# HGRN2 recurrence of a hybrid decoder step: the operands of levels 4, 8 and of the first corner copied aside, the level products grouped

## The chip, the cores and the metric

The kernel runs on one core of a Trainium2 chip. The metric is the device time of one execution in microseconds (us), median of the runs. All work is in one program: products on TensorE (PE), elementwise work on VectorE (DVE) and ScalarE (ACT), a little on GpSimd (POOL), and transfers issued mostly by SyncE (SP).

## What is computed

The reference is one step of a two-layer decoder for a prompt of 2048 tokens and 8 sample sequences of 8 tokens. Layer 0 joins a gated DeltaNet with sliding-window attention; layer 1 is an HGRN2 recurrence with 8 heads of 128 x 128 state. The change touches layer 1 alone:

```python
def hgrn2_recurrence(q, k, v, logf, s0):
    # S_t = diag(f_t) S_{t-1} + k_t v_t^T (k_t = 1 - f_t), o_t = S_t^T q_t / sqrt(dk), chunkwise
    ...
    def step(s, xs):
        q_c, k_c, v_c, G_c = xs
        dec = masked_exp(causal, G_c[:, :, :, None, :] - G_c[:, :, None, :, :])
        a = jnp.einsum('nhid,nhijd,nhjd->nhij', q_c, dec, k_c)
        o = jnp.einsum('nhid,nhde->nhie', q_c * jnp.exp(G_c), s) + jnp.einsum('nhij,nhje->nhie', a, v_c)
        gl = G_c[:, :, -1]
        s = s * jnp.exp(gl)[..., None] + jnp.einsum('nhid,nhie->nhde', k_c * jnp.exp(gl[:, :, None] - G_c), v_c)
        return s, o
```

Here `a` is a causal matrix of token by token, in which each pair is damped by the forget gates of the tokens between them, channel by channel.

## The kernel before

All operands of the large products are split into a high and a low part, so that a product is three passes (`product`). These are the **dense** products. They write three PSUM banks (bank_66 to bank_68); everything else writes five more (bank_69 to bank_73).

Layer 1 is done in **units**: one head and a group of token tiles of 128. `GROUPS[1]` has, in its first half, groups of 4, 2 (with the 64 sample tokens beside them) and 2 tiles, and in its second half two of 4. With 8 heads these are 24 units of four tiles and 16 of two. For a unit `dense_hgrn` (dense stream) makes the products for the gate, q and the output gate; `gates` and `silu2` empty them; `hgrn_unit` then runs the recurrence, with `hgrn_core` building the causal matrix A, and `hgrn_sample` does so for the sample tokens.

`hgrn_core` builds A by levels. At level s the tokens lie in blocks of 2s; q of a block's right half and k of its left half carry the decay to the border between them, and their product is that level's part of A.

- Level 1, level 2 and the diagonal are sums over channels of elementwise products, done by PE with a matrix of ones (`sums`).
- Levels 4, 8 and 16 are products of 32 tokens by 32 tokens (`prod`), one for each 32 rows of a tile, of which a mask keeps the level's part (`copy_predicated` with `m4`, `m8`, `m16`).
- Levels 32 and 64 are the corners of A: two products of 32 x 32 and one of 64 x 64 per tile.

Between two levels DVE scales q and k **in place** by the decays (three operations: right halves of q, left halves of k, the block decays B). So the product of one level has to have read k and q before the next scaling may start. In PE's array these products use a small tile: the profile writes 128*32 (32 columns of weights) or 128*64 for them, and 128*128 for the dense products. A product in f32 leaves two records in the trace.

Nothing of the order is written by hand. All the stages are generators (threads) that yield their next operation, and `Sched.run` writes into the program, at each step, the operation that its own bookkeeping says can start first; the dense stream has a lower claim and fills what is left. Each engine then works off its own queue in that order. Up to `UNITS[2]` = 3 units of layer 1 are under way. A unit reserves 7 times its width plus `RH` columns of an arena of 50 blocks of 1024 columns before its dense products start, and the dense stream waits for that.

All instructions carry the line of the scheduler's helper (L354), so the views are read by tiles and shapes.

Of the kernel before, what the change touches and what calls it, by code (L numbers as in the profile page):

```python
# [46 lines left out]
FIRSTW, LASTG, WO0, WO1, GB = 30, 12, 6, 8, 2  # L47
PREP, WG0 = 2, 1
DMARGIN = 0
RD, RH = 8, 256  # L50
NBLK = 50
UNITS = (6, 5, 3)
XBUDGET = [18, 20]
# [499 lines left out]
def al(n, r=False):  # L553

    return Ask("mem", (n, r))
# [22 lines left out]
class Step(Sched):  # L578
# [1134 lines left out]
        u["f"], u["k"] = e1, e2  # L1713
        self.dirty = True

    def hgrn_core(self, np_, n, cs, q, k, f, levels, out, own):
# [12 lines left out]

        def prod(ps, qq):  # L1730

            for c in range(n):
                for r in range(nb):
                    t = slice(c * cs + 32 * r, c * cs + 32 * r + 32)
                    yield self.P.matmul(out=ps[rows[r], c * 32 : c * 32 + 32], lhsT=k[:, t], rhs=qq[:, t], start=True, stop=True)

        def sums(ps, c0, x, w):

            xv = x.rearrange("p (c r i) -> p c r i", r=nb, i=w)
            for r in range(nb):  # L1740
# [9 lines left out]
        for s in levels + (2 * levels[-1],):  # L1750
            if s > 1:
                hs, nbk = s // 2, W // s
                qv = QF.rearrange("p (b r i) -> p b r i", r=2, i=hs)
                kv = k.rearrange("p (b r i) -> p b r i", r=2, i=hs)
                bv = B.rearrange("p (b r) -> p b r", r=2)
                yield self.V.tensor_tensor(out=qv[:, :, 1, :], in0=qv[:, :, 1, :], in1=bc(bv[:, :, 0], 2, hs), op=ALU.mult)
                yield self.V.tensor_tensor(out=kv[:, :, 0, :], in0=kv[:, :, 0, :], in1=bc(bv[:, :, 1], 2, hs), op=ALU.mult)
                if Bs is None:
                    Bs = yield al(W)
                B = Bs[:, bo : bo + nbk]  # L1760
                bo += nbk
                yield self.V.tensor_tensor(out=B, in0=bv[:, :, 0], in1=bv[:, :, 1], op=ALU.mult)
                if s == 2 and own:
                    self.free(f)
            if s > levels[-1]:
                break
            if s == 1:
                continue
            ps = yield bank()
            if s == 2:  # L1770
                Q4, K4, P4 = cut(QF, 4), cut(k, 4), kdb[:, :W].rearrange("p (b j i) -> p b j i", j=2, i=2)
                for j in range(2):
                    yield self.V.tensor_tensor(out=P4[:, :, j, :], in0=Q4[:, :, 2:4], in1=bc(K4[:, :, j], 2, 2), op=ALU.mult)
                yield from sums(ps, n * 48, Ab, 32)
                yield from sums(ps, 0, P1[:, : W // 2], 16)
                yield from sums(ps, n * 16, kdb[:, :W], 32)
                yield self.V.tensor_tensor(out=Dv, in0=cut(ps[:np_, n * 48 : n * 80], 32), in1=bc(self.c("ident32")[:np_], 1, n), op=ALU.mult)
                yield self.G.memset(ap=Ab[:np_], constant=0.0)
                D2, D4 = Dv.rearrange("p c (b i) -> p c b i", i=2), Dv.rearrange("p c (b i) -> p c b i", i=4)
                yield self.V.copy_predicated(out=D2[:, :, :, 1], mask=bc(cut(self.c("m1")[:np_], 2)[:, :, 1].bitcast(U32), 1, n), data=cut(ps[:np_, : n * 16], 16))  # L1780
                for j in range(2):
                    d = ps[:np_, n * 16 : n * 48].rearrange("p (c b j i) -> p c b j i", b=8, j=2, i=2)[:, :, :, j, :]
                    yield self.V.copy_predicated(out=D4[:, :, :, 2:4], mask=bc(cut(self.c(("m2", "m2o")[j])[:np_], 4)[:, :, 2:4].bitcast(U32), 1, n), data=d)
                self.free(P1)
            elif s <= 16:
                yield from prod(ps, QF)
                yield self.V.copy_predicated(out=Dv, mask=bc(self.c(f"m{s}")[:np_].bitcast(U32), 1, n), data=cut(ps[:np_, : n * 32], 32))
            else:

                cor = [(j, s) for j in range(0, 128, 2 * s)]  # L1790
                for c in range(n):
                    for j, _ in cor:
                        t = c * cs + j
                        yield self.P.matmul(out=ps[j : j + s, c * s : (c + 1) * s], lhsT=k[:, t : t + s], rhs=QF[:, t + s : t + 2 * s], start=True, stop=True)
                for j, _ in cor:
                    yield self.A.activation(out=A[j : j + s, :, j + s : j + 2 * s], in_=cut(ps[j : j + s, : n * s], s), func=AF.Copy)
# [12 lines left out]
    def hgrn_unit(self, half, h, hh, gi, u, vs):  # L1809
# [50 lines left out]
    def hgrn_sample(self, h, q, k, f, v, sg):  # L1860
# [284 lines left out]
```

## Time and profile before

| what | value |
|---|---|
| median of 3 runs | 3143.66 us (3141.78 to 3158.1) |
| the profiled execution | 3148.57 us |
| its span, first to last instruction | 3146.8 us |
| granted PE clock, mean | 0.983 |
| PE busy | 3054.1 us, 97% |
| weight loads (PEld) busy | 2507.9 us, 80% |
| DVE busy | 1962.1 us, 62% |
| ACT busy | 1149.5 us, 37% |
| layer 1's recurrence, about 1625 to 2700 us: PE / DVE / ACT busy | 1052.9 / 772.0 / 375.1 of 1075 us |

In a timeline row the columns are: start in us, length in us, engine, line, operation, names of what is written and read, tile mode and shape, and the number of instructions merged; a wait ahead of it stands in brackets with what ended it. A row of groups ends with busy us, mean ns of one, and idle us before them. In a row of waits: total us, times, longest us. A row of windows: the stretch, its length, busy us of each engine in the order of its header, the granted clock, the share of DMA time and GB/s.

### The profile page before, as it was taken

What the parts mean: (1) busy time and instruction counts of PE and PEld (TensorE: products, weight loads), DVE (VectorE), ACT (ScalarE), POOL (GpSimd) and SP (SyncE); (2) the same over time, 40 slices, a digit from 0 to 9 for tenths busy, and PEclk for the clock granted to TensorE, in tenths of its full rate; (3) what the DMA queues carried; (4) which work ended last, traced back from release to release, by engine and by line L of the source; (5) the groups of instructions that cost most, each with busy time, mean ns of one, the idle gap of its engine ahead of it and who ended that gap; (6) DMA issues with size and microseconds to landing.
All of it is one profiled execution on the core that took longest, in us unless ns stands there. A gap on an engine that the chain in (4) does not pass through costs nothing.

```text
span 3146.8 us, 63372 instructions
## 1 busy us (share of the span) xinstructions
PE 3054.1 (97%) x25592; PEld 2507.9 (80%) x25592; DVE 1962.1 (62%) x5693; ACT 1149.5 (37%) x3074; POOL 197.1 (6%) x265
## 2 busy tenths in 40 slices
PE   8999899999999999999999999998999999999999
PEld 7787777877877787878888888786888888787787
DVE  5567776776757674333457686868577576733333
ACT  4455454655555561111143332324333333311011
POOL 0000000000000001111000000000000000111110
PEclk9999999999989999999999999999999999999999
DMA  4231222321214264233322122213111121732331
GB/s 118 70 86 41 59 69 61 95 63 47 81 48 121 77 174 107 75 82 89 104 74 69 42 69 67 65 56 99 56 52 52 46 69 49 221 87 75 82 86 49
DMA packets 320837, 246.45 MB, mean 78 GB/s; under 512 B 33800, under 2 KB 285840, under 8 KB 320528
## 3 DMA queue, kind: packets, MB, share of 16 engines
q1 hardware_dynamic: 253408, 207.80, 21.8%
q0 software_dynamic: 67136, 34.61, 6.1%
q8 instruction: 201, 3.29, 0.4%
q14 instruction: 92, 0.75, 0.1%
HBM read 182.98 MB, written 60.45 MB: 77 GB/s over the span
## 4 chain that ended last, share of the span: by engine, by line
PE 57%; DVE 7%; DMA 4%; issue 3%; ACT 2%; POOL 0%; SPq 0%; POOLq 0%; DVEq 0%; ACTq 0%
PE bank L354 57%; DVE ar L354 7%; DMA ar<-in_w_in_odd 2%; ACT ar L354 2%; DMA ar<-in_w_in_even 1%; POOL ar L354 0%; SPq L354 0%; DMA ar<-gd 0%; DMA ar<-in_w_ple_gate 0%; DMA ar<-x 0%; DMA os<-ar 0%; ACT L354 0%; DMA ar<-in_w_out_even 0%; DMA ctail<-ar 0%; DMA gd<-ar 0%
## 5 line engine op out<-in xcount | busy, mean ns | idle before, releaser
L354 PE MATMUL bank<-ar,ar 128*128 128x512 f32 (+10 forms) x20168 | 2865.9, 306 | 55.5 <-DVE ar L354 30.8
L354 PEld LDWEIGHTS bank<-ar,ar 128*128 128x128 f32 (+4 forms) x20168 | 2250.9, 163 | 490.4 <-issue 85.8
L354 ACT ACTIVATE ar<-bank 128x128 f32<-128x128 f32 (+13 forms) x1471 | 528.0, 369 | 1343.8 <-PE bank L354 1250.5
L354 DVE TENSOR_TENSOR ar<-ar,ar 128x256 f32<-128x256 f32 (+9 forms) x1517 | 737.1, 514 | 245.2 <-ACT ar L354 207.5
L354 ACT ACTIVATE ar<-ar 128x1024 fp32r<-128x1024 f32 (+12 forms) x833 | 443.1, 551 | 581.7 <-DMA ar<-in_pT 248.6
L354 DVE SCALAR_TENSOR_TENSOR ar<-ar,bank 128x512 f32<-128x512 f32 (+3 forms) x256 | 164.1, 641 | 393.4 <-ACT ar L354 261.6
L354 PE MATMUL bank<-cst,ar 128*128 128x128 f32 (+4 forms) x1439 | 244.2, 280 | 21.1 <-DVE ar L354 14.7
L354 PEld LDWEIGHTS bank<-cst,ar 128*128 128x128 f32 (+4 forms) x1439 | 172.9, 141 | 72.4 <-issue 19.0
L354 DVE TENSOR_TENSOR ar<-bank,ar 128x128 fp32r<-128x128 f32 (+7 forms) x326 | 147.6, 455 | 80.7 <-ACT ar L354 45.2
L354 POOL TENSOR_TENSOR ar<-ar,mhalf 128x2 f32<-128x2 f32 (+3 forms) x104 | 107.6, 1035 | 1361.6 <-DVE ar L354 978.5
L354 DVE TENSOR_TENSOR ar<-ar 128x256 f32<-128x256 f32 (+11 forms) x575 | 135.6, 248 | 15.4 <-ACT ar L354 14.1
L354 DVE SCALAR_TENSOR_TENSOR ar<-bank,ar,ar 128x509 f32<-128x509 f32 (+8 forms) x216 | 123.0, 573 | 26.2 <-ACT ar L354 24.7
L354 DVE COPY_PREDICATED ar<-cst,bank 128x128 f32<-128x128 uint32 (+4 forms) x356 | 93.0, 262 | 72.7 <-PE bank L354 61.5
L354 PEld LDWEIGHTS bank<-ar 128*32 128x32 f32 (+4 forms) x2904 | 90.5, 121 | 45.5 <-DVE ar L354 17.9
L354 PE MATMUL bank<-ar 128*32 128x32 f32 (+5 forms) x2904 | 116.8, 212 | 8.2 <-DVE ar L354 6.9
L354 DVE SCALAR_TENSOR_TENSOR ar<-ar,ar,bank 128x128 f32<-128x128 f32 x192 | 65.7, 342 | 74.1 <-PE bank L354 72.6
L354 POOL MEMSET ar<- 128x256 f32 (+4 forms) x85 | 29.0, 348 | 1141.7 <-PE bank L354 772.8
L354 DVE SCALAR_TENSOR_TENSOR ar<-ar,ar,ar 128x1024 f32<-128x1024 f32 (+1 forms) x68 | 87.0, 1279 | 13.4 <-POOL ar L354 13.3
L354 POOL DMA_DIRECT2D ar<-os x64 | 57.4, 898 | 283.1 <-PE bank L354 214.1
L354 DVE SCALAR_TENSOR_TENSOR ar<-ar,ar 128x512 f32<-128x512 f32 (+10 forms) x187 | 55.9, 304 | 30.4 <-ACT ar L354 29.1
L354 DVE TENSOR_SCALAR ar<-bank 128x512 f32<-128x512 f32 (+2 forms) x80 | 44.6, 592 | 36.2 <-ACT ar L354 35.8
L354 ACT ACTIVATION_READ_ACCUMULATOR ar<-bank 128x1 f32 (+1 forms) x340 | 66.4, 195 | 0.2
(55 smaller groups left out, 820.7 us busy)
## 6 DMA issues: line engine op xcount, KB each, us to landing
ar<-os POOLq DMA_DIRECT2D x64, 512.0 KB, 4.9
ar<-in_w_in_odd SPq DMA_DIRECT2D x64, 512.0 KB
ar<-in_w_in_even SPq DMA_DIRECT2D x60, 512.0 KB
os<-ar SPq DMA_DIRECT2D x36, 512.0 KB
ar<-x SPq DMA_DIRECT2D x32, 512.0 KB
os<-ar SPq DMA_DIRECT2D x56, 256.0 KB
ar<-in_x_prompt SPq DMA_DIRECT2D x16, 512.0 KB
ar<-in_w_ple_gate SPq DMA_DIRECT2D x16, 512.0 KB
```

What stands on the lines that cost most here:

```text
L354: o.fn = lambda: f(**kw)
```

## The change

In `hgrn_core`, which now takes `deep` (true for the prompt, false for the samples, which need levels 1 to 4 alone):

- The scaling between two levels becomes a helper, `scale(s)`. The products of level 2's sums (P4) are formed before any of the sums is issued, so all three sums stand together.
- Before the scaling for level 8, ACT copies all of k and the right halves of q aside (KA, QA); before that for level 16, again (KB, QB). Level 16 uses k and q in place. The three levels' products are then issued one after the other into one bank.
- Only the right halves' columns are multiplied: 16 columns per 32 tokens instead of 32. `level` lays them out, with half of the mask.
- For the first corner ACT copies the left halves of k and the right halves of q (KC, QC) into KB, so that its products can be issued with those of the 64 corner after the scaling for 64. Both share a bank, and ACT empties them after the last scaling.
- For the samples, level 4 goes into the bank of the sums.
- `RH` goes from 256 to 512.

So each unit of the prompt has three groups of small products: the sums, the levels, the corners. The number of products is the same as before. The diff, cut to its core:

```diff
-RD, RH = 8, 256
+RD, RH = 8, 512
...
-        def prod(ps, qq):
+        def scale(s):
...
+            yield self.V.tensor_tensor(out=qv[:, :, 1, :], in0=qv[:, :, 1, :], in1=bc(bv[:, :, 0], 2, hs), op=ALU.mult)
+            yield self.V.tensor_tensor(out=kv[:, :, 0, :], in0=kv[:, :, 0, :], in1=bc(bv[:, :, 1], 2, hs), op=ALU.mult)
...
+            yield self.V.tensor_tensor(out=B, in0=bv[:, :, 0], in1=bv[:, :, 1], op=ALU.mult)
+
+        def prod(ps, c0, kk, qq):
...
-                    t = slice(c * cs + 32 * r, c * cs + 32 * r + 32)
-                    yield self.P.matmul(out=ps[rows[r], c * 32 : c * 32 + 32], lhsT=k[:, t], rhs=qq[:, t], start=True, stop=True)
+                    t = c * cs + 32 * r
+                    yield self.P.matmul(out=ps[rows[r], c0 + c * 16 : c0 + c * 16 + 16], lhsT=kk[:, t : t + 32], rhs=qq(c * nb + r), start=True, stop=True)
+
+        def level(ps, c0, s):
+
+            d = Dv.rearrange("p c (b r i) -> p c b r i", r=2, i=s)[:, :, :, 1, :]
+            m = self.c(f"m{s}")[:np_].rearrange("p (b r i) -> p b r i", r=2, i=s)[:, :, 1, :]
+            x = ps[:np_, c0 : c0 + n * 16].rearrange("p (c b i) -> p c b i", c=n, i=s)
+            yield self.V.copy_predicated(out=d, mask=bc(m.bitcast(U32), 1, n), data=x)
...
+            ps = yield bank()
+            yield from sums(ps, n * 48, Ab, 32)
+            yield from sums(ps, 0, P1[:, : W // 2], 16)
+            yield from sums(ps, n * 16, kdb[:, :W], 32)
...
-            elif s <= 16:
-                yield from prod(ps, QF)
-                yield self.V.copy_predicated(out=Dv, mask=bc(self.c(f"m{s}")[:np_].bitcast(U32), 1, n), data=cut(ps[:np_, : n * 32], 32))
-            else:
-
-                cor = [(j, s) for j in range(0, 128, 2 * s)]
-                for c in range(n):
-                    for j, _ in cor:
-                        t = c * cs + j
-                        yield self.P.matmul(out=ps[j : j + s, c * s : (c + 1) * s], lhsT=k[:, t : t + s], rhs=QF[:, t + s : t + 2 * s], start=True, stop=True)
-                for j, _ in cor:
-                    yield self.A.activation(out=A[j : j + s, :, j + s : j + 2 * s], in_=cut(ps[j : j + s, : n * s], s), func=AF.Copy)
...
+            KA, QA = kdb, P1
+            ops = []
+            for s, kk, qq in ((4, KA, QA), (8, KB, QB)):
+                yield self.A.activation(out=kk[:, :W], in_=k, func=AF.Copy)
+                yield self.A.activation(out=cut(qq[:, : W // 2], s), in_=right(QF, s), func=AF.Copy)
+                ops.append((kk, cut(qq[:, : W // 2], 16)))
+                yield from scale(2 * s)
             ps = yield bank()
...
+            for i, (kk, qq) in enumerate(ops):
+                yield from prod(ps, i * n * 16, kk, lambda b: qq[:, b])
+            q16 = right(QF, 16)
+            yield from prod(ps, 2 * n * 16, k, lambda b: q16[:, b])
+            self.free(P1, QB)
+            yield from scale(32)
+
+            KC, QC = (cut(KB[:, i * W // 2 : (i + 1) * W // 2], 32) for i in range(2))
+            yield self.A.activation(out=KC, in_=k.rearrange("p (b r i) -> p b r i", r=2, i=32)[:, :, 0, :], func=AF.Copy)
+            yield self.A.activation(out=QC, in_=right(QF, 32), func=AF.Copy)
+            for i, s in enumerate((4, 8, 16)):
+                yield from level(ps, i * n * 16, s)
             self.freebank(ps)
+            yield from scale(64)
+            ps = yield bank()
+            for c in range(n):
+                for b in range(2):
+                    yield self.P.matmul(out=ps[64 * b : 64 * b + 32, c * 32 : (c + 1) * 32], lhsT=KC[:, 2 * c + b], rhs=QC[:, 2 * c + b], start=True, stop=True)
+            for c in range(n):
+                t = c * cs
+                yield self.P.matmul(out=ps[0:64, n * 32 + c * 64 : n * 32 + (c + 1) * 64], lhsT=k[:, t : t + 64], rhs=QF[:, t + 64 : t + 128], start=True, stop=True)
+            self.free(KB)
+            yield from scale(128)
+            for j in (0, 64):
+                yield self.A.activation(out=A[j : j + 32, :, j + 32 : j + 64], in_=cut(ps[j : j + 32, : n * 32], 32), func=AF.Copy)
+            yield self.A.activation(out=A[0:64, :, 64:128], in_=cut(ps[0:64, n * 32 : n * 96], 64), func=AF.Copy)
+            self.freebank(ps)
...
-        yield from self.hgrn_core(128, nt, 128, q[:, :Wp], k[:, :Wp], f[:, :Wp], SMALL + (32, 64), r, not smp)
+        yield from self.hgrn_core(128, nt, 128, q[:, :Wp], k[:, :Wp], f[:, :Wp], True, r, not smp)
...
-        yield from self.hgrn_core(ST, 1, ST, q, k, f, (1, 2, 4), r, False)
+        yield from self.hgrn_core(ST, 1, ST, q, k, f, False, r, False)
```

More of the change, by code (lines that the diff above doesn't have):

```diff
@@ L1714, in gates, with hgrn_core @@
         self.dirty = True
-    def hgrn_core(self, np_, n, cs, q, k, f, levels, out, own):
+    def hgrn_core(self, np_, n, cs, q, k, f, deep, out, own):
         W = n * cs
@@ L1728, in hgrn_core, with right @@
         B = f
-        def prod(ps, qq):
+        def scale(s):
+            nonlocal B, Bs, bo
+            hs, nbk = s // 2, W // s
+            qv = QF.rearrange("p (b r i) -> p b r i", r=2, i=hs)
+            kv = k.rearrange("p (b r i) -> p b r i", r=2, i=hs)
+            bv = B.rearrange("p (b r) -> p b r", r=2)
+            yield self.V.tensor_tensor(out=qv[:, :, 1, :], in0=qv[:, :, 1, :], in1=bc(bv[:, :, 0], 2, hs), op=ALU.mult)
+            yield self.V.tensor_tensor(out=kv[:, :, 0, :], in0=kv[:, :, 0, :], in1=bc(bv[:, :, 1], 2, hs), op=ALU.mult)
+            if Bs is None:
+                Bs = yield al(W)
+            B = Bs[:, bo : bo + nbk]
+            bo += nbk
+            yield self.V.tensor_tensor(out=B, in0=bv[:, :, 0], in1=bv[:, :, 1], op=ALU.mult)
+        def prod(ps, c0, kk, qq):
             for c in range(n):
                 for r in range(nb):
-                    t = slice(c * cs + 32 * r, c * cs + 32 * r + 32)
-                    yield self.P.matmul(out=ps[rows[r], c * 32 : c * 32 + 32], lhsT=k[:, t], rhs=qq[:, t], start=True, stop=True)
+                    t = c * cs + 32 * r
+                    yield self.P.matmul(out=ps[rows[r], c0 + c * 16 : c0 + c * 16 + 16], lhsT=kk[:, t : t + 32], rhs=qq(c * nb + r), start=True, stop=True)
+        def right(x, s):
+            return x.rearrange("p (b r i) -> p b r i", r=2, i=s)[:, :, 1, :]
+        def level(ps, c0, s):
[3 more added lines that the diff above has]
+            yield self.V.copy_predicated(out=d, mask=bc(m.bitcast(U32), 1, n), data=x)
         def sums(ps, c0, x, w):
@@ L1749, in hgrn_core @@
         yield self.V.tensor_tensor(out=P1[:, : W // 2], in0=Q2[:, :, 1], in1=K2[:, :, 0], op=ALU.mult)
[L1750 to L1768, printed above, removed]
-            ps = yield bank()
[L1770 to L1784, printed above, removed]
-            elif s <= 16:
-                yield from prod(ps, QF)
-                yield self.V.copy_predicated(out=Dv, mask=bc(self.c(f"m{s}")[:np_].bitcast(U32), 1, n), data=cut(ps[:np_, : n * 32], 32))
-            else:
-                cor = [(j, s) for j in range(0, 128, 2 * s)]
-                for c in range(n):
-                    for j, _ in cor:
-                        t = c * cs + j
-                        yield self.P.matmul(out=ps[j : j + s, c * s : (c + 1) * s], lhsT=k[:, t : t + s], rhs=QF[:, t + s : t + 2 * s], start=True, stop=True)
-                for j, _ in cor:
-                    yield self.A.activation(out=A[j : j + s, :, j + s : j + 2 * s], in_=cut(ps[j : j + s, : n * s], s), func=AF.Copy)
-            self.freebank(ps)
@@ new lines, in hgrn_core @@
+        yield from scale(2)
+        if own:
+            self.free(f)
+        Q4, K4, P4 = cut(QF, 4), cut(k, 4), kdb[:, :W].rearrange("p (b j i) -> p b j i", j=2, i=2)
+        for j in range(2):
+            yield self.V.tensor_tensor(out=P4[:, :, j, :], in0=Q4[:, :, 2:4], in1=bc(K4[:, :, j], 2, 2), op=ALU.mult)
+        if deep:
+            KB = yield al(W)
+            QB = yield al(W // 2)
+        else:
+            yield from scale(4)
+        ps = yield bank()
+        yield from sums(ps, n * 48, Ab, 32)
@@ new lines, in hgrn_core @@
+        yield from sums(ps, 0, P1[:, : W // 2], 16)
+        yield from sums(ps, n * 16, kdb[:, :W], 32)
+        if deep:
+            yield from scale(4)
+        else:
+            q4 = QF.rearrange("p (g b r i) -> p g b r i", b=4, r=2, i=4)[:, :, :, 1, :]
+            yield from prod(ps, n * 80, k, lambda b: q4[:, b])
+        yield self.V.tensor_tensor(out=Dv, in0=cut(ps[:np_, n * 48 : n * 80], 32), in1=bc(self.c("ident32")[:np_], 1, n), op=ALU.mult)
+        yield self.G.memset(ap=Ab[:np_], constant=0.0)
@@ new lines, in hgrn_core @@
+        D2, D4 = Dv.rearrange("p c (b i) -> p c b i", i=2), Dv.rearrange("p c (b i) -> p c b i", i=4)
+        yield self.V.copy_predicated(out=D2[:, :, :, 1], mask=bc(cut(self.c("m1")[:np_], 2)[:, :, 1].bitcast(U32), 1, n), data=cut(ps[:np_, : n * 16], 16))
+        for j in range(2):
+            d = ps[:np_, n * 16 : n * 48].rearrange("p (c b j i) -> p c b j i", b=8, j=2, i=2)[:, :, :, j, :]
+            yield self.V.copy_predicated(out=D4[:, :, :, 2:4], mask=bc(cut(self.c(("m2", "m2o")[j])[:np_], 4)[:, :, 2:4].bitcast(U32), 1, n), data=d)
@@ new lines, in hgrn_core @@
+        if not deep:
+            yield from level(ps, n * 80, 4)
+            yield from scale(8)
+        self.freebank(ps)
+        if deep:
+            KA, QA = kdb, P1
[5 more added lines that the diff above has]
+                yield from scale(2 * s)
+            ps = yield bank()
+            for i, (kk, qq) in enumerate(ops):
[9 more added lines that the diff above has]
+                yield from level(ps, i * n * 16, s)
+            self.freebank(ps)
+            yield from scale(64)
[11 more added lines that the diff above has]
+            yield self.A.activation(out=A[0:64, :, 64:128], in_=cut(ps[0:64, n * 32 : n * 96], 64), func=AF.Copy)
+            self.freebank(ps)
+        else:
+            self.free(P1)
```

## Prediction

> **What bounds the kernel now.** The page first: its engines and the chain that ended last.
>
> ```profile
> span 3146.8 us, 63372 instructions
> PE 3054.1 (97%) x25592; PEld 2507.9 (80%) x25592; DVE 1962.1 (62%) x5693; ACT 1149.5 (37%) x3074; POOL 197.1 (6%) x265
> PE 57%; DVE 7%; DMA 4%; issue 3%; ACT 2%; POOL 0%; SPq 0%; POOLq 0%; DVEq 0%; ACTq 0%
> ```
>
> PE is busy for 97% of the span and leads the chain. The change lies in layer 1's recurrence, so I read that stage next, by the windows and by the waits within them (from 1625 us, where the first unit's small products begin, to 2700 us).
>
> ```profile
> core 0: us, PE busy (x) PEld busy (x) DVE busy (x) ACT busy (x) POOL busy (x), PEclk, DMA share, GB/s
> 1625.00:2700.00 1075.00, 1052.90 (x10504) 879.32 (x10503) 771.98 (x2366) 375.06 (x1000) 62.14 (x105) 0.99 0.22 64
> ```
> ```profile
> PE bank L354 <- DVE ar L354: 20.2, 28, 2.2
> PE bank L354 <- DMA ar<-x: 0.4, 1, 0.4
> ```
>
> PE is idle for only 1075.00 - 1052.90 = 22.1 us of the stage, nearly all of it behind DVE. DVE has 28% of the stage free and ACT 65%. So nothing but PE's own time, or a new wait of PE, can move the end by much. A busy PE is not a PE at its peak, though: the page models the ends of matmuls. What a short stretch of small products costs must be read from starts, in the timeline of PE. Here are a two-tile unit and then a four-tile unit.
>
> ```profile
> 1660.73 2.42 PE L354 MATMUL bank<-ar,ar 128*128 128x256 f32 x18
> 1663.08 0.33 PE L354 MATMUL bank<-ar 128*32 128x32 f32 x16
> 1663.34 1.70 PE L354 MATMUL bank<-ar,ar 128*128 128x256 f32 x12
> 1664.97 0.33 PE L354 MATMUL bank<-ar 128*32 128x32 f32 x16
> 1665.23 1.70 PE L354 MATMUL bank<-ar,ar 128*128 128x256 f32 x12
> ...
> 1635.52 2.05 PE L354 MATMUL bank<-ar,ar 128*128 128x256 f32 x15
> 1637.50 0.46 PE L354 MATMUL bank<-ar 128*32 128x32 f32 x32
> 1637.89 2.06 PE L354 MATMUL bank<-ar,ar 128*128 128x256 f32 x15
> ```
>
> From start to start, 18 dense matmuls and a stretch of 16 small records take 1663.34 - 1660.73 = 2.61 us; 12 dense and such a stretch take 1665.23 - 1663.34 = 1.89 us. Six dense matmuls are therefore 0.72 us, 0.120 us each, and the stretch costs 1.89 - 12 x 0.120 = 0.45 us. In the four-tile unit, 15 dense and 32 records take 1637.89 - 1635.52 = 2.37 us; the stretch costs 2.37 - 15 x 0.120 = 0.57 us. So 16 more records add 0.12 us (7.5 ns each), and **each visit to the small tile mode costs 0.45 - 0.12 = 0.33 us, whatever is done in it**. (A product in f32 leaves two records.)
>
> **The change, part by part.**
>
> *Fewer visits.* In before each level's product must be done before DVE may scale k and q in place for the next level, so levels 4, 8 and 16 are three visits. Now copies hold the operands of 4 and 8, and the products are issued together. PE's order around the first four-tile unit, as a difference (bank_67 takes the dense product; bank_72 is now the bank of the three levels, ar_15565 and ar_15589 hold copied keys, ar_15503 copied queries, ar_15504 is k):
>
> ```order
>  L354 MATMUL bank_67<-ar_14954,ar_15268 128x256
> +L354 MATMUL bank_72<-ar_15565 32x16 x16
> +L354 MATMUL bank_72<-ar_15503,ar_15589 32x16 x16
>  L354 MATMUL bank_67<-ar_14953,ar_15271 128x256
> +L354 MATMUL bank_72<-ar_15504 32x16 x16
>  L354 MATMUL bank_67<-ar_14953,ar_15268 128x256
>  L354 MATMUL bank_67<-ar_14954,ar_15268 128x256
> -L354 MATMUL bank_73<-ar_15504 32x32 x16
> ```
>
> Levels 4 and 8 have become one visit, but the scheduler puts one dense matmul between them and level 16: two visits where there were three, not one. It does so in most units. So I counted the whole program: from layer 1 on, PE leaves its 128x128 mode and comes back 355 times before and 284 times after, 71 visits fewer; layer 0 is the same in both. All changes of mode in the program go from 1497 to 1375, 122 fewer; 71 visits are 142 changes, so in 20 places two small modes now follow each other directly (the corners 32 and 64 above all). The sums keep their two visits per unit.
>
> - 71 visits x 0.33 us = -23.4 us.
> - 20 direct changes: no row isolates one. It is free at best; at worst it costs half of a visit's two changes, 0.17 us. I take the worst, since it too ends one mode and begins another: +3.4 us.
>
> The Trainium skill, "TensorEngine Tiling (Array Packing)", section Key Properties, says that a change of mode, not of tile, drains the engine, which speaks against counting a corner that follows a corner as free; no row here shows such a pair alone. By that rule the +3.4 us stay; without it the sum would be 3.4 us lower.
>
> *Half the columns.* Each level product now writes 16 columns instead of 32. Do records get shorter? Two rows of equal count, and four of the timeline:
>
> ```profile
> L354 PE MATMUL bank<-ar,ar 128*64 128x8 f32 x128 | 11.7, 218 | 0.0
> L354 PE MATMUL bank<-ar 128*64 128x64 f32 x128 | 11.7, 230 | 5.1 <-DVE ar L354 5.1
> ```
> ```profile
> 1687.80 0.26 PE L354 MATMUL bank<-ar,cst 128*32 128x32 f32 x4
> 1687.99 0.49 PE L354 MATMUL bank<-ar,ar 128*128 128x512 f32 x1
> 1688.41 0.24 PE L354 MATMUL bank<-ar,cst 128*32 128x16 f32 x4
> 1688.58 0.50 PE L354 MATMUL bank<-ar,ar 128*128 128x512 f32 x1
> ```
>
> 128 records of 8 columns keep PE busy exactly as long as 128 of 64 columns, 11.7 us: the width does not set the time there. Four records of 32 columns reach the next dense start after 0.19 us, four of 16 after 0.17 us: 0.02 us at the end of a visit. Some 80 visits will end so: -1.6 us. The other bound is a record at half the 7.5 ns: there are 24 x 96 + 16 x 48 = 3072 level records (24 units of four tiles, 16 of two), so -11.5 us; I keep it as a rival.
>
> The Trainium skill's page "TensorEngine Tiling (Array Packing)", section Instruction Overhead, says that a matmul with one column lasts as long as one with 60 and warns against shrinking what is already small. By that rule this part gives nothing, and the equal 11.7 us agree; by the halving the sum would be about 10 us lower.
>
> *Copies on ACT.* ACT's order at the same unit, as a difference (ar_15504 is k, ar_15565 and ar_15589 copies; rows that read a bank empty PE's results):
>
> ```order
>  L354 ACTIVATE ar_15460<-bank_71 128x128 x4
> -L354 ACTIVATE ar_15589<-bank_66 128x512
> -L354 ACTIVATE ar_15565<-bank_68 128x256
> -L354 ACTIVATE ar_15503<-bank_67 128x256
> -L354 ACTIVATE ar_15503<-bank_71 32x4x32 x2
> +L354 ACTIVATE ar_15565<-ar_15504 128x512
> +L354 ACTIVATE ar_15565<-ar_15504 128x256
> +L354 ACTIVATE ar_15622<-bank_66 128x512
> +L354 ACTIVATE ar_15589<-ar_15504 128x512
> +L354 ACTIVATE ar_15503<-ar_15504 128x256
> +L354 ACTIVATE ar_15503<-bank_68 128x256
> +L354 ACTIVATE ar_15589<-ar_15504 128x256 x2
> ```
>
> Six copies per unit stand between the rows that empty the dense banks. Nearest rows:
>
> ```profile
> L354 ACT ACTIVATE ar<-ar 128x512 f32<-128x512 f32 x108 | 65.4, 627 | 38.0 <-DVE ar L354 37.1
> L354 ACT ACTIVATE ar<-ar 128x256 f32<-128x256 f32 x74 | 30.9, 432 | 13.5 <-DVE ar L354 13.4
> L354 ACT ACTIVATE ar<-ar 32x128 f32<-32x128 f32 x72 | 21.7, 301 | 7.1 <-DVE ar L354 6.5
> ```
>
> Four tiles: 2 x 0.63 + 4 x 0.43 = 2.98 us, times 24 = 71.5 us; two tiles: 2 x 0.43 + 4 x 0.30 = 2.06 us, times 16 = 33 us. ACT goes from 375 to about 480 us of the 1075: off the path. What they add is a wait: DVE may scale k for level 8 only once ACT has copied it (1.06 us for a four-tile level), where it used to wait for PE's product. Behind that scaling on DVE stand the next gates and weight splits. Dense products of the following units cover it; I cost it at nothing, and its uncovered price is the slower rival.
>
> *Smaller DVE work.* The predicated copies of the three levels take half the elements.
>
> ```profile
> L354 DVE COPY_PREDICATED ar<-cst,bank 128x128 f32<-128x128 uint32 x120 | 35.9, 299 | 43.0 <-PE bank L354 38.8 <-ACT ar L354 2.0 <-issue 0.8
> L354 DVE COPY_PREDICATED ar<-cst,bank 128x64 f32<-128x64 uint32 x152 | 39.7, 261 | 25.8 <-PE bank L354 22.7 <-ACT ar L354 0.2
> ```
>
> 24 x 3 x 0.038 = 2.7 us off DVE, hidden beside PE.
>
> *Memory.* A unit reserves 256 columns more, 768 for three, of 51,200. The dense stream waits for that reservation. In the order no longer stretch without dense products appears, save the one at the turn of the halves (70 small products before, 80 after). Nothing is booked for it.
>
> *Sum.* -23.4 + 3.4 - 1.6 = -21.6; a few of the visits stand at that turn, where PE waits anyway, so -21 us. The profiled execution took 3148.57 us (span 3146.8 and 1.8 around it), which makes 3127.6; it lies 4.9 us above the median of 3143.66, and on that median the sum gives **3123 us**, 0.67% less. About 0.5%, 15.7 us, is what a measurement of this kernel can tell from no change.
>
> **The rivals.**
>
> *16 columns halve a record.* For it: the stream is half as long. Against: the two equal rows. It would give -21 - 10 = -31 us, 3113 us.
>
> *PE's waits behind DVE shrink too.* Products from copies are not urgent for DVE's next step, so the 20.2 us above could halve: 3113 us as well. Against: those waits come from DVE and ACT being late for other reasons (next rows), which the change leaves.
>
> *The gain is partly eaten.* If the visits that went were those at which PE was about to run dry, or the reservation holds the dense stream now and then, a third to two thirds of the 21 us come back: 3130 to 3137 us, within 0.5%.
>
> *Slower: ACT late for a weight holds the copies.* One place where a weight split holds ACT, and then DVE and PE:
>
> ```profile
> 1670.76 1.06 ACT L354 ACTIVATE ar<-ar 128x1024 fp32r<-128x1024 f32 x1 [3.65 <-DMA ar<-in_w_in_odd]
> 1671.85 1.63 DVE L354 TENSOR_TENSOR ar<-ar,ar 128x1024 fp32r<-128x1024 f32 x3 [3.89 <-ACT ar L354]
> 1673.54 0.45 PE L354 MATMUL bank<-ar 128*64 128x64 f32 x4 [1.89 <-DVE ar L354]
> ...
> ACT ar L354 <- DMA ar<-in_w_in_odd: 39.2, 28, 3.7
> ```
>
> In the stage ACT waits 39.2 us, 28 times, for weights still on their way. Copies queued behind such a split would be late, DVE's scaling and then PE's products with them. If all 39.2 us reached PE: 39.2 - 21 = +18, 3162 us. It decides once PE's waits in the stage rise from 22 us past 43. Against: DVE is held at the same split already (3.89 us above), and PE lost just 1.89 us there.
>
> That the change does not do what it says is partly settled: three runs per unit are not what the order shows, and the sum uses what it shows.
>
> **How the numbers follow.** Forecast 0.64 (3123, with some 6 us either way for waits that fall elsewhere in a new order: 3117 to 3129), halved records 0.06, shorter waits 0.09, partly eaten 0.14, slower 0.07. The line of 0.5% lies at 3128: four fifths of the forecast and both quicker rivals are beyond it, 0.51 + 0.15 = 0.66; a fifth of the forecast and the eaten case give 0.27; slower 0.07. The range leaves out the slower rival and the far ends of the quick ones: 3106 to 3143.
>
> **What would show it.** In the profile of the changed kernel, PE's timeline should show stretches of 64 records of 128x16 that cost 0.33 + 64 x 0.0075 = 0.81 us, and of 32 that cost 0.55 to 0.57; PE's idle time in the recurrence 16 to 28 us; ACT about 105 us busier; the stage some 20 us shorter, with layer 0 and the last stage unchanged. The forecast is wrong if a 64-record stretch costs under 0.65 us (the columns count), if PE's waits there pass 35 us (ACT or DVE is the bound), or if the stage keeps its length with fewer visits (a visit was hidden by something else).

## The result and the profile after

Five runs of the changed kernel have a median of 3131.6 us (3127.57 to 3131.8), five of the kernel before, beside them, 3147.03 us: a ratio of 0.9944 with a 95% interval of 0.9925 to 0.9964, or 15.4 us by the medians (the ratio is worth 17.6 us, 11 to 24). Measured again later, with 12 runs, the ratio was 0.9959 (0.9945 to 0.9974). So the change is faster, by about half a per cent.

The page of the changed kernel, its span and its engines:

```profile
span 3129.8 us, 63577 instructions
PE 3036.5 (97%) x25592; PEld 2500.8 (80%) x25592; DVE 1963.1 (63%) x5693; ACT 1231.4 (39%) x3314; POOL 199.7 (6%) x265
```

PE executes as many instructions as before and is as full as before, 97%; it is 17.6 us less busy, and the span is 17.0 us shorter. ACT is 82 us busier. The same stretch of the recurrence by the windows (columns as before), and PE's waits in it:

```profile
1625.00:2700.00 1075.00, 1052.11 (x10642) 885.73 (x10641) 785.24 (x2395) 461.17 (x1243) 66.61 (x108) 0.99 0.23 68
```
```profile
PE bank L354 <- DVE ar L354: 17.1, 25, 1.6
PE bank L354 <- ACT ar L354: 4.0, 11, 0.8
PE bank L354 <- DMA ar<-x: 0.2, 1, 0.2
```

PE idles 1075.00 - 1052.11 = 22.9 us where it idled 22.1, and the named waits sum to 21.3 us instead of 20.6: no wait went away. In the same 1075 us it gets through 10642 instructions instead of 10504: the gain lies in how closely its instructions follow each other. The timeline of PE shows it. First the first four-tile unit (64 records of levels 4 and 8, one dense matmul among the 33 of the middle row, 32 records of level 16), then two visits with one dense matmul between them, then one visit of a two-tile unit:

```profile
1632.52 0.45 PE L354 MATMUL bank<-ar 128*32 128x16 f32 x32
1632.80 0.78 PE L354 MATMUL bank<-ar,ar 128*32 128x16 f32 x33
1633.50 0.45 PE L354 MATMUL bank<-ar 128*32 128x16 f32 x32
1633.88 2.65 PE L354 MATMUL bank<-ar,ar 128*128 128x256 f32 x20
...
2478.58 0.46 PE L354 MATMUL bank<-ar 128*32 128x16 f32 x32
2478.97 0.38 PE L354 MATMUL bank<-ar,ar 128*128 128x256 f32 x1
2479.29 0.44 PE L354 MATMUL bank<-ar 128*32 128x16 f32 x32
...
1660.14 0.32 PE L354 MATMUL bank<-ar 128*32 128x16 f32 x16
1660.39 2.17 PE L354 MATMUL bank<-ar,ar 128*128 128x256 f32 x16
1662.49 0.32 PE L354 MATMUL bank<-ar 128*32 128x32 f32 x8
```

From the first record of a visit to the next dense start, 16 records take 1660.39 - 1660.14 = 0.25 us and 32 take 1633.88 - 1633.50 = 0.38 us. The 64 take 1633.50 - 1632.52 = 0.98 us together with the dense matmul after them; that matmul up to the next visit takes 2479.29 - 2478.97 = 0.32 us, which leaves 0.66 us. What comes before the first record and after the return is in the last pair of rows: 16 dense matmuls of 0.120 us would be 1.92 us, and 2.10 pass. These 0.18 us belong to each visit too, so the stretches cost 0.43, 0.56 and 0.84 us. Forecast were 0.55 to 0.57 for the 32 and 0.81 for the 64.

For the sum over the program I matched each product of PE's order with its record in the trace, and compared the starts of the same dense products before and after. Up to the first dense product of layer 1, where both programs are the same, the changed kernel is 4.1 us ahead. The trace's record of the granted clock has only two values, full and half, and up to that point it is at half for 85 us in the execution before and for 75 us in the one after; that is a difference between two executions and not one of the change. The recurrence takes 1101.9 us where it took 1114.8: **-12.9 us**. Behind it nothing changes. In the second profile of the changed kernel it took 1107.4 us, so one profile fixes this number to some 5 us. The 12.9 us by kind (distances are from start to start, counted by what they exceed the usual one between equal products):

| what | measured | in the prediction |
|---|---|---|
| entering and leaving visits, and the dense matmuls just after (71 visits fewer, 16 columns at the exits) | -21.6 | -25.0 |
| small mode to small mode (20 more) | +2.6 | +3.4 |
| inside the visits, distances with no idle time of 0.1 us | +4.3 | none |
| other dense matmuls | +2.5 | none |
| PE idle, waits of 0.1 us and over | -1.0 | none |
| left over | +0.3 | |

Two of these terms can be followed further in the traces. Of the 4.3 us, about 1 us lies at products for which a semaphore was released within the distance; for the rest the trace names no wait, so what they are stays open. Of the 2.5 us in other dense matmuls, about 2 lie in stretches at half clock: these sum to 21.8 us of the recurrence, against 17.1 before. In the second profile of the changed kernel they sum to 31.1 us, and 3.8 of the 5.5 us that lie between the two profiles are dense matmuls in them.

ACT's copies and DVE's predicated copies in the changed kernel, by shape over the whole program:

```profile
L354 ACT ACTIVATE ar<-ar 128x512 f32<-128x512 f32 x156 | 96.2, 628 | 102.3 <-DVE ar L354 101.4
L354 ACT ACTIVATE ar<-ar 128x256 f32<-128x256 f32 x202 | 80.8, 417 | 76.7 <-DVE ar L354 76.0
L354 ACT ACTIVATE ar<-ar 128x128 f32<-128x128 f32 x66 | 18.1, 297 | 15.4 <-DVE ar L354 15.4
```
```profile
L354 DVE COPY_PREDICATED ar<-cst,bank 128x64 f32<-128x64 uint32 x176 | 45.2, 257 | 16.4 <-PE bank L354 12.1 <-ACT ar L354 0.2
L354 DVE COPY_PREDICATED ar<-cst,bank 128x128 f32<-128x128 uint32 x48 | 14.3, 299 | 13.7 <-PE bank L354 10.6 <-ACT ar L354 2.1 <-issue 0.8
```

The first two ACT rows have 48 and 128 instructions more than their rows of before, and the third is nearly all new; 30.8 + 49.9 + 17.5 = 98 us of copies (0.6 us of the third row stood there before). ACT's busy time rose by only 82 us: all its groups together rose by 96, but their times overlap. ACT waits for DVE ahead of them. In exchange DVE waits less for PE's level products: ahead of the predicated copies of these two shapes it idled 43.0 + 25.8 = 68.8 us, and now 16.4 + 13.7 = 30.1. Its waits for PE as a whole shrink less. Before and after, in the stage:

```profile
DVE ar L354 <- PE bank L354: 152.0, 151, 4.1
```
```profile
DVE ar L354 <- PE bank L354: 138.3, 104, 5.0
```

That DVE passes the levels without waiting for PE is what the copies buy at once; what it is worth to PE is the question of the experiments.

### The profile page after: what moved, and what is told of

It reads as the page before. It is cut to its first block, busy times and chain, and to the rows that moved or that the text cites. A ratio compares the mean times of both kernels' runs of the same rounds, so it can differ in the third digit from the quotient of the medians.

```text
span 3129.8 us, 63577 instructions
## 1 busy us (share of the span) xinstructions
PE 3036.5 (97%) x25592; PEld 2500.8 (80%) x25592; DVE 1963.1 (63%) x5693; ACT 1231.4 (39%) x3314; POOL 199.7 (6%) x265
## 3 DMA queue, kind: packets, MB, share of 16 engines
q1 hardware_dynamic: 253408, 207.80, 22.1%
## 5 line engine op out<-in xcount | busy, mean ns | idle before, releaser
L354 PE MATMUL bank<-ar,ar 128*128 128x512 f32 (+9 forms) x20656 | 2851.5, 301 | 50.6 <-ACT ar L354 24.7
L354 DVE TENSOR_TENSOR ar<-ar,ar 128x256 f32<-128x256 f32 (+10 forms) x1473 | 729.8, 523 | 255.5 <-ACT ar L354 211.3
L354 ACT ACTIVATE ar<-ar 128x256 f32<-128x256 f32 (+13 forms) x1073 | 530.5, 522 | 738.0 <-DVE ar L354 376.0
L354 DVE TENSOR_TENSOR ar<-ar 128x4 f32<-128x4 f32 (+10 forms) x619 | 142.4, 246 | 16.6 <-ACT ar L354 14.2
L354 PEld LDWEIGHTS bank<-ar 128*32 128x32 f32 (+3 forms) x2416 | 89.4, 123 | 39.5 <-issue 14.4
L354 PE MATMUL bank<-ar 32*32 32x32 f32 (+6 forms) x2416 | 114.2, 211 | 5.4 <-ACT ar L354 3.7
L354 DVE COPY_PREDICATED ar<-cst,bank 128x64 f32<-128x64 uint32 (+4 forms) x356 | 85.9, 242 | 35.0 <-PE bank L354 22.7
L354 DVE SCALAR_TENSOR_TENSOR ar<-ar,ar,ar 128x1024 f32<-128x1024 f32 (+1 forms) x68 | 87.0, 1280 | 13.7 <-POOL ar L354 13.6
```

The source lines that it names most:

```text
L354: o.fn = lambda: f(**kw)
```

## The experiments

The theory on trial is that of the prediction: a visit to the small mode has a price of its own, whatever is done in it, and the copies cost nothing because dense products cover them. Rivals: the columns count; the copies themselves (operands early) bring the gain; ACT's new work eats part of it; PE runs dry when visits are merged. The visits are counted in PE's order (whole program; 707 before). Ratios are to the kernel before, run beside each.

| run | edit | visits | median us | ratio (95%) |
|---|---|---|---|---|
| a1_after_again | none | 636 | 3134.73 | 0.9959 (0.9945 to 0.9974) |
| e1_cols32 | 32 columns | 636 | 3133.78 | 0.9957 (0.9939 to 0.9975) |
| e2_split | copies, but a visit per level | 690 | 3145.28 | 0.9991 (0.9977 to 1.0005) |
| e8_extra_visits | 104 useless visits | 740 | 3162.83 | 1.0050 (1.0036 to 1.0065) |
| e5_copies_twice | each copy done twice | 640 | 3142.57 | 0.9986 (0.9973 to 1.0000) |
| e11_corners_apart | first corner as before | 649 | 3136.80 | 0.9979 (0.9961 to 0.9997) |
| e4_before_stay1000 | kernel before, handicap 1000 | 623 | 3151.80 | 1.0021 (1.0008 to 1.0034) |
| e6_stay400 | handicap 400 | 589 | 3122.69 | 0.9934 (0.9918 to 0.9950) |
| e3_stay1000 | handicap 1000 | 515 | 3111.36 | 0.9888 (0.9867 to 0.9910) |
| e9_stay2000 | handicap 2000 | 495 | 3150.18 | 1.0011 (0.9996 to 1.0027) |
| e10_stay3000 | handicap 3000 | 453 | 3251.17 | 1.0332 (1.0314 to 1.0350) |
| e7_all_stay1000 | handicap 1000 in both layers | 430 | 3124.91 | 0.9937 (0.9921 to 0.9953) |

**The changed kernel again** (a1_after_again), as the yardstick for the others.

> The changed kernel once more, beside the others on one chip. Both theories: 3127 to 3133 us, 15 to 18 us under the kernel before.

It came out at 0.9959. The runs below are set against this value.

**Do the columns count?** (e1_cols32) Each level product gets 32 columns again, in the same order; the second 16 are not used.

```diff
-                    yield self.P.matmul(out=ps[rows[r], c0 + c * 16 : c0 + c * 16 + 16], lhsT=kk[:, t : t + 32], rhs=qq(c * nb + r), start=True, stop=True)
+                    w, o = (32, -16 * (deep and c * nb + r == n * nb - 1)) if deep else (16, 0)
+                    yield self.P.matmul(out=ps[rows[r], c0 + c * w + o : c0 + c * w + o + w], lhsT=kk[:, t : t + 32], rhs=qq(c * nb + r), start=True, stop=True)
```

> The changed kernel with 32 columns in each level product again (the instructions stand in the same order on every engine, only the width differs). Theory 'a visit to the small tile mode has a fixed price and the columns do not count': 1 us slower than the changed kernel (some 90 visits end 0.013 us later), so within its noise. Rival 'half the columns is where the gain comes from': 10 to 12 us slower than the changed kernel (3072 records at half of 7.5 ns).

The times are equal, 0.9957 and 0.9959. The group of these records in the stage, in the changed kernel and here:

```profile
L354 PE MATMUL bank<-ar,ar 128*32 128x16 f32 x2512 | 36.3, 186 | 1.6 <-ACT ar L354 0.8 <-DVE ar L354 0.3
```
```profile
L354 PE MATMUL bank<-ar,ar 128*32 128x32 f32 x2496 | 36.8, 200 | 1.6 <-ACT ar L354 0.8 <-DVE ar L354 0.3
```

The mean length of a record rises by 14 ns, but about 2500 of them keep PE busy equally long, since each starts long before the one ahead of it ends. By starts the width shows only at the end of a visit: from its last record to the next dense start pass 113 ns with 16 columns and 126 ns with 32 (medians), which over the program is about 1 us. The time doesn't follow the columns otherwise; the rival of the halved records, 10 to 12 us, falls, since the two intervals leave room for 7 us.

**Is it the copies or the visits?** (e2_split) Copies and 16 columns stay, but each level's products are issued and read before the next scaling.

```diff
-                ops.append((kk, cut(qq[:, : W // 2], 16)))
+                qc = cut(qq[:, : W // 2], 16)
+                ps = yield bank()
+                yield from prod(ps, 0, kk, lambda b: qc[:, b])
+                yield from level(ps, 0, s)
+                self.freebank(ps)
                 yield from scale(2 * s)
```

> The changed kernel with the copies and the 16 columns kept, but each level's product issued and masked as soon as its own copies are made, so three visits for the levels again. PE then leaves its 128x128 mode 690 times in the program instead of 636 (before: 707). Theory 'visits': 54 more at 0.27 to 0.33 us each, 14 to 18 us slower than the changed kernel, 3144 to 3150 us, no quicker than the kernel before by more than 5 us. Rival 'the copies free DVE and the chain': stays within 4 us of the changed kernel.

54 of the 71 visits are back, and 0.32% of the time with them: 10 us, 0.19 per visit, a little under the theory's 14 to 18 and over the rival's 4; with the two intervals it is 4 to 16 us. The kernel is about as slow as before (0.9991), with all the copies in it. DVE waits for PE ahead of its predicated copies as before, 46.7 us in this row against 12.1:

```profile
L354 DVE COPY_PREDICATED ar<-cst,bank 128x64 f32<-128x64 uint32 x176 | 45.0, 256 | 49.3 <-PE bank L354 46.7 <-ACT ar L354 0.2
```

So copies without grouping bring nothing that can be told from zero. But this run takes away two things at once: the visits are back, and DVE again waits for PE at each level, since a level's masked copy stands ahead of the next scaling. It does not show what DVE's freedom alone would be worth. The next run leaves that freedom and adds visits.

**The price of a visit by itself** (e8_extra_visits). 116 useless products of 16 columns are strewn ahead of dense products; nothing reads them.

```diff
+            if extra is not None and k == 0:
+                yield self.P.matmul(out=extra, lhsT=self.c("ones")[:, 0:32], rhs=self.c("ones")[:, 0:16], start=True, stop=True)
```

> The changed kernel with one useless product of 128 x 32 by 128 x 16 constants (two records, nobody reads it) put ahead of each dense product of layer 1 that leaves room in its bank: 116 of them, 104 of which are a visit of their own (740 visits instead of 636), the other 12 fall into one that is there already. Its operands are always ready, so no wait is in it. Theory 'a visit costs 0.33 us': 104 x 0.33 = 34 us slower than the changed kernel, 30 to 37. Rival 'a visit costs what the grouping brought for each one removed, 0.17 to 0.19 us': 18 to 20 us slower.

104 more visits (the others fell beside one that was there). The difference in ratio is 0.91%, 28.6 us, or 0.275 us a visit; with the two intervals (0.15% either way each, 0.21% together, 6.6 us), 0.21 to 0.34. One of them in the timeline:

```profile
1799.88 0.39 PE L354 MATMUL bank<-ar,ar 128*128 128x320 f32 x1
1800.20 0.23 PE L354 MATMUL bank<-cst 128*32 128x16 f32 x2
1800.37 4.43 PE L354 MATMUL bank<-ar,ar 128*128 128x320 f32 x30
```

Two records, and 0.17 us pass before the next dense start; the rest of the price lies in front and behind. The starts agree: 100 of the 104 visits lie in the recurrence, and the ends of visits take 29 us more there than in the changed kernel. So a visit has a price of its own, nearer to 0.28 us than to the theory's 0.33; the rival's 18 to 20 us lie outside the interval.

**Are the copies free?** (e5_copies_twice) Each of the six copies is done twice.

```diff
-                yield self.A.activation(out=kk[:, :W], in_=k, func=AF.Copy)
-                yield self.A.activation(out=cut(qq[:, : W // 2], s), in_=right(QF, s), func=AF.Copy)
+                for _ in range(2):
+                    yield self.A.activation(out=kk[:, :W], in_=k, func=AF.Copy)
+                    yield self.A.activation(out=cut(qq[:, : W // 2], s), in_=right(QF, s), func=AF.Copy)
```

> The changed kernel with each of the six copies on ACT done twice (the second writes the same again). ACT gets some 104 us more; PE's visits are 640 instead of 636. Theory 'the copies are hidden': 0 to 4 us slower than the changed kernel. Rival 'ACT holds DVE and PE, and the copies eat part of the gain': a tenth or more of the added time reaches PE, 10 us slower or more.

0.27% slower, 8.5 us, with 4 visits more (1 us); with the two intervals 2 to 15 us, so between the theory's 4 and the rival's 10 and not clear of either. PE's waits in the stage:

```profile
PE bank L354 <- DVE ar L354: 25.0, 40, 4.5
PE bank L354 <- ACT ar L354: 4.5, 11, 0.9
PE bank L354 <- DMA ar<-in_state_hgrn_c: 3.5, 3, 1.6
PE bank L354 <- DMA ar<-x: 1.3, 1, 1.3
```

They are 34.3 us against 21.3: 7.9 of the 13 us are behind DVE, 4.6 behind transfers. DVE waits for ACT longer:

```profile
DVE ar L354 <- ACT ar L354: 151.8, 172, 3.6
```

In the changed kernel that row reads

```profile
DVE ar L354 <- ACT ar L354: 112.5, 153, 3.6
```

(DVE's waits for PE fall by as much, from 138.3 to 95.6 us.) So the chain that the prediction described, copy, then scaling, then PE, can account for some 8 us of PE's waits, though ACT has half the stage free. What the first set of copies costs inside the measured gain is not isolated by this.

**The corner** (e11_corners_apart). The first corner's products are issued after the scaling for 32, without copies, as before.

```diff
-            KC, QC = (cut(KB[:, i * W // 2 : (i + 1) * W // 2], 32) for i in range(2))
-            yield self.A.activation(out=KC, in_=k.rearrange("p (b r i) -> p b r i", r=2, i=32)[:, :, 0, :], func=AF.Copy)
-            yield self.A.activation(out=QC, in_=right(QF, 32), func=AF.Copy)
+            pc = yield bank()
+            for c in range(n):
+                for b in range(2):
+                    t = c * cs + 64 * b
+                    yield self.P.matmul(out=pc[64 * b : 64 * b + 32, c * 32 : (c + 1) * 32], lhsT=k[:, t : t + 32], rhs=QF[:, t + 32 : t + 64], start=True, stop=True)
```

> The changed kernel with the first corner done as before (its products straight from k and q, before the scaling for 64, in a bank of its own): four copies per unit on ACT instead of six, 649 visits instead of 636. Theory 'visits and copies': 13 visits more at 0.27 us cost 3.5 us, a third of the copies less gives up to 3 us: within 4 us of the changed kernel. Rival 'the corner is a large part of the gain': 6 us slower or more.

0.9979 against 0.9959; the intervals overlap. Two copies fewer per unit and 13 visits more come out even or somewhat worse; inconclusive.

**More of the same** (e3_stay1000, e6_stay400). In the scheduler's choice a dense product that would end a visit is put back by `STAY` = 40 ns. In layer 1 this handicap becomes 1000 or 400. The work is the same, only the order changes.

```diff
-                    s -= SWITCH[o.mode == WHOLE] - STAY * (o.mode == WHOLE)
+                    s -= SWITCH[o.mode == WHOLE] - (self.stay if hasattr(self, "stay") else STAY) * (o.mode == WHOLE)
...
         if half == 0:
+            self.stay = 1000
```

> The changed kernel with the scheduler's handicap for going back to the 128x128 mode raised from 40 to 1000 in layer 1, so that small products already close to ready are gathered first. PE leaves the 128x128 mode 515 times instead of 636. Theory 'visits': 121 fewer at 0.27 to 0.33 us, 33 to 40 us quicker than the changed kernel, about 3095 us, if PE never stands waiting in the small mode. Rival 'what fewer visits give is taken back by waits': PE's waits in the recurrence grow from 21 us to 50 or more and the time stays at 3125 us or above.

> The changed kernel with the handicap at 400 in layer 1: 589 visits, between the changed kernel's 636 and the 515 of the run with 1000. Theory 'visits': 47 fewer at 0.17 to 0.27 us net, 8 to 13 us quicker than the changed kernel, 3120 to 3126 us. Rival 'it is the waits that decide': no order by visits, the time lies outside 3116 to 3130.

589 and 515 visits, 0.9934 and 0.9888: 8 and 22 us faster than the changed kernel (7 us either way). With 1000 the three levels of the first unit are one visit:

```profile
1632.27 0.45 PE L354 MATMUL bank<-ar 128*32 128x16 f32 x32
1632.54 0.43 PE L354 MATMUL bank<-ar,ar 128*32 128x16 f32 x30
...
1632.84 0.46 PE L354 MATMUL bank<-ar 128*32 128x16 f32 x30
1633.23 2.51 PE L354 MATMUL bank<-ar,ar 128*128 128x256 f32 x19
```

96 records reach the next dense start in 0.96 us. PE's instructions in the stage, and its waits:

```profile
1625.00:2700.00 1075.00, 1044.37 (x10718) 896.12 (x10717) 798.59 (x2416) 466.90 (x1261) 69.91 (x112) 0.99 0.24 72
```
```profile
PE bank L354 <- DVE ar L354: 22.0, 48, 1.6
PE bank L354 <- ACT ar L354: 7.8, 8, 2.2
```

By the matched starts, 191 visits fewer than before (the stretch holds all but one of the 192) save 51.4 us at their ends, 0.27 each; of that 10.3 come back as distances inside the visits, of which the trace shows almost 4 as waits that a semaphore ended, 4.3 in other matmuls and 4.1 as idle time. The expectation of 33 to 40 us below the changed kernel was the full price times the visits; some 60% of it came. The rival's waits of 50 us did not come either: PE idles 30.6 us. **This order beats both kernels.**

**The same handicap without copies** (e4_before_stay1000): the kernel before, with that edit.

> The kernel before, with nothing of the change, but the scheduler's handicap for going back to the 128x128 mode in layer 1 raised from 40 to 1000. PE leaves the 128x128 mode 623 times (before: 707, the changed kernel: 636), with 32 columns, no copies and each level's product made before the next scaling. Theory 'visits': 84 fewer at 0.17 to 0.27 us net, 14 to 23 us quicker than before, 3124 to 3133 us, about the changed kernel's time. Rival 'the copies, which let DVE go on while products wait, are what brings the gain': above 3141 us, no better than 6 us under the kernel before, since PE then stands waiting for operands that can't be put aside.

84 visits fewer than before, and not faster: 1.0021. At the ends of visits 22.6 us are saved, 0.27 each again, but idle time grows by 16.7 us and the distances inside visits by 9.9 (about 4 of them waits that a semaphore ended):

```profile
1625.00:2700.00 1075.00, 1036.19 (x10484) 874.74 (x10485) 768.89 (x2357) 369.32 (x989) 65.13 (x106) 0.98 0.23 65
```
```profile
PE bank L354 <- DVE ar L354: 29.5, 47, 1.6
PE bank L354 <- DMA ar<-os: 7.7, 2, 7.3
```

Of the idle time, 11 us more than before lie between two small products, where PE waits for DVE to scale the next level; 7.3 us are one wait for a transfer at the end of the stage. Other dense matmuls take over 4 us more, most of it at half clock (34 us of the recurrence against 17); whether the order causes that was not tried.

This is the second half of the answer. Visits can be merged without copies, but then PE stands in the small mode and waits. With the copies (e3) it stands there about as long, 19.9 us between small products against 17.8, but for 192 visits fewer and not 84. The same handicap merges more than twice as much for the same waiting where operands are put aside. A smaller handicap without the copies was not tried.

**Where it ends** (e9_stay2000, e10_stay3000, e7_all_stay1000). The same edit with 2000 and 3000 in layer 1, and with 1000 in both layers.

> The changed kernel with the handicap at 2000 in layer 1: 495 visits (with 1000: 515). Theory 'visits': 20 fewer at 0.17 to 0.27 us, 3 to 5 us under the run with 1000, about 3107 us. Rival 'waits take over': PE's waits in the recurrence pass 35 us and the time is 3113 us or above.

> The changed kernel with the handicap at 3000 in layer 1: 453 visits. Theory 'visits': 62 fewer than with 1000, at 0.17 us or more each: 3101 us or less. Rival 'waits take over': what PE waits for operands in the small mode grows by more than the 17 us that the visits give at most, and the time is above 3115 us.

> The changed kernel with the handicap at 1000 in both layers: 430 visits, 85 fewer than with 1000 in layer 1 alone, all of them in layer 0. Theory 'visits': 85 at 0.17 to 0.27 us net, 14 to 23 us quicker than the run with 1000 in layer 1 (3111 us), about 3093 us. Rival 'layer 0's chains of small products make PE wait': PE's idle time in layer 0 grows by 15 us or more and the time is 3108 us or above.

495 visits give 1.0011, 453 give 1.0332. The stage of both, by windows and waits, first with 2000:

```profile
1625.00:2700.00 1075.00, 1026.09 (x10575) 884.34 (x10574) 773.28 (x2377) 454.05 (x1235) 66.51 (x107) 0.97 0.23 66
```
```profile
PE bank L354 <- DVE ar L354: 38.0, 53, 2.4
PE bank L354 <- DMA ar<-os: 8.7, 2, 8.2
```

With 3000:

```profile
1625.00:2700.00 1075.00, 966.34 (x9566) 838.78 (x9565) 707.50 (x2186) 413.00 (x1134) 55.28 (x96) 0.92 0.19 54
```
```profile
PE bank L354 <- ACT ar L354: 60.6, 41, 2.3
PE bank L354 <- DVE ar L354: 45.1, 78, 1.9
```

PE idles 49 us in the first and 109 us in the second, there half of it behind ACT; with 1000 it was 30.6. Both pass the lines that the expectations drew for their rivals. But the waits are not all of it. The granted clock is 0.97 and 0.92 where it was 0.99: half clock takes 75 and 191 us of the recurrence, with 1000 it took 30. From start to end the recurrence is 33 and 138 us longer than with 1000, and idle time accounts for 22 and 89 us of that. The rest is put down to the clock and to short waits inside the visits, since fewer visits alone would shorten it; no run varies the clock by itself.

In layer 0 there are no such copies. With the handicap in both layers the recurrence is nearly as short as in e3 (1086.1 us against 1082.3), but layer 0 takes 15 us longer than before and 20 longer than in e3. PE idles 16 us more than in e3 there, as the rival said:

```profile
PE bank L354 <- ACT ar L354: 39.9, 40, 7.3
```

With 1000 in layer 1 alone that row of layer 0 reads

```profile
PE bank L354 <- ACT ar L354: 23.0, 21, 7.4
```

Half clock is 106 us there against 75. The profiled execution was the longest of its six, 10 us over their median, so the difference by the medians is smaller.

## Why the prediction was right, and where its terms were off

The forecast was 3123 us (3106 to 3143), and the time is 3131.6: inside the range, and in microseconds where the rival "the gain is partly eaten" put it. Part of that is the yardstick: the forecast stood on 3143.66 us for the kernel before, which took 3147.03 beside the changed one. As a gain, 17.6 us by the ratio (11 to 24) do not tell the forecast's 15 to 27 from the rival's 7 to 14; the second measurement, 0.9959 or 12.9 us, and the traces speak for the rival. The mechanism was right, and the sum was too large: -12.9 us in the recurrence by the profile, and -15.4 us by the medians, where it had -21.

- *Fewer visits.* 71 went, as counted in the order. Their price, read from three stretches of one timeline, was 0.33 us; the ends of all visits give 21.6 / 71 = 0.30 with the shorter exits in it, and 19.0 / 71 = 0.27 with the direct changes paid. The ends of visits in e3 and e4 give 0.27 too, and the added visits of e8 0.275 by time.
- *Direct changes.* 2.6 / 20 = 0.13 us each, near the worst case that was taken (0.17). They are not free, in agreement with the rule of the Trainium skill, "TensorEngine Tiling (Array Packing)", Key Properties, that a change of mode drains.
- *Half the columns.* Right: next to nothing. e1 has the same time with 32. The -1.6 us booked for the ends of visits was 0.02 us each; the starts give 0.013. The Trainium skill, "TensorEngine Tiling (Array Packing)", section Instruction Overhead, says that a matmul with one column lasts as long as one with 60. The distances inside a visit agree, four records starting every 31 to 32 ns with either width; its end does not quite, 113 ns against 126, and there the measurement decides.
- *Copies on ACT.* The step "cover it; I cost it at nothing" was the weak one. The size was right (98 us of instructions against 104.5), and PE's waits in the stage did not grow, 21.3 us against 20.6, where the slower rival needed over 43. But the cover is thin: in e5 as much again costs 8.5 us (2 to 15), and PE's waits behind DVE grow by 7.9 us, as the path named there would have it. ACT's busy time rose by 82 us, where about 105 were forecast.
- *What the sum left out.* Inside the merged visits the distances grew by 4.3 us, and other dense matmuls by 2.5. The first looks like the rival's condition, that grouped products come while PE is close to running dry, but the trace shows only about 1 us of it as waits; e3 and e4, with about 4 of some 10 us each, show such waits clearly. Of the second about 2 us are half clock. The rival's second condition, a reservation that holds the dense stream, falls: with `RH` at 256 again the program is the same, instruction by instruction.
- *The stage.* Forecast some 20 us shorter, measured 12.9 and, in the second profile, 7.4. Idle time was forecast at 16 to 28 us and is 22.9.
- *Waits behind DVE shrink too.* They hardly did: 17.1 us behind DVE instead of 20.2, but 4.0 behind ACT that were not there before.

Open stays how much of the 6.8 us given back is due to the copies' lateness, how much to the grouping itself and how much to the clock; no run does one without the other, and two profiles of one kernel differ by 5.5 us in the stage, mostly by the clock.

## What to carry to other kernels

Count in the instruction order how often TensorE leaves its large tile mode, and take the price of one visit from starts, with the first dense matmuls after the return in it; busy time doesn't show it. Grouping small products pays only as far as their operands are ready: put the operands aside on an engine with room, and then tell the scheduler to use them, since here the unchanged handicap left more on the table (0.9888 against 0.9959) than the change itself took. Stop where the time turns, which was between 515 and 495 visits here: PE's idle time and its time at half clock grew together beyond that, and cost more than the visits gave.

## What the runs showed of the hardware

- The second dense matmul after a return starts about 0.10 us late, besides about 0.09 at the entry and 0.11 at the exit (medians from starts, in the kernels before and after): a third of a visit's price lies behind it, where one would not look for it. A dense matmul of 256 columns alone between two visits takes 0.32 us instead of 0.12.
- Records of the 128*32 mode start every 7.5 to 8 ns on average, whether they have 16 or 32 columns: rounds of four start 31 to 32 ns apart in the changed kernel and in e1.
- The granted clock is full or half, and half comes in stretches of 3.4 us and multiples of it. In the recurrence it made up 17 us before, 22 and 31 us in two executions of the changed kernel, 75 us in e9 and 191 us in e10, where PE idled 109 us of the stage. Why it fell was not tried.
- The time follows this clock from one execution to the next of the same program: over the 71 executions of the kernel before that were run beside the experiments, 0.001 less of the mean granted clock goes with some 2.7 us more.
